# An encoder's self-attention output projection: seven block products with left sums summed in memory, in place of a plain product

## The chip, the cores and the metric

The kernel runs on one core of one Trainium2 chip. The metric is the device time of one execution in microseconds (us): the median of three runs before the change is 2370.38 us (2369.58 to 2371.14). One execution was also profiled; it took 2370.06 us, of which 2368.3 us are the span that the profile shows, so 1.8 us lie around it.

Five engines work side by side, each with its own instruction queue that runs in order: PE (TensorE, matrix products, with its weight loads shown as PEld), DVE (VectorE), ACT (ScalarE), POOL (GpSimd) and SP (SyncE, which here only issues transfers). Sixteen DMA engines move the data of the transfers.

## The reference, cut to what matters

A two-layer encoder over 1024 tokens of 1024 channels, all in float32. Layer 0 mixes tokens by self-attention, layer 1 by a pooling mixer; each layer then attends to 256 memory tokens and runs a gated feed-forward part.

```python
def axial_gqa_attention(h, w_qkv, q_gain, k_gain, w_o):
    qkv = h @ w_qkv                      # 16 query heads of 64, 4 key/value heads
    ...
    o = softmax(q k^T) v                 # for each head, 1024 x 64
    return o @ w_o                       # (1024 x 1024) @ (1024 x 1024)

def memory_cross_attention(h, mem_n, w_q, w_kv, w_o):
    q, kv = h @ w_q, mem_n @ w_kv        # mem_n: 256 x 1024, w_kv: 1024 x 2048
    ...

x = x + axial_gqa_attention(rmsnorm(x, g), ...)
x = x + memory_cross_attention(rmsnorm(x, g), ...)
x = x + conv_gated_ffn(rmsnorm(x, g), ...)
```

## The kernel before

**Arithmetic.** A float32 operand is kept as a high part (fp32r, cut by an ACT copy, helper `high`, L620) and a low part (the rest, a DVE subtraction, helper `low`, L623). A product of two such operands takes three matrix instructions (helper `mm3`, L696 to L698: high by high, high by low, low by high). Split operands live in 20 slots `R` of 128 x 2048 numbers, each of two halves. Float32 data on its way is held in a few scratch tiles `scr` of 128 x 1024.

**Stages.** First w_qkv is applied (to 155 us of the span), then attention runs (155 to 428 us), then attention's output projection (`attention_out`, L1944), then layer 0's cross-attention with its query projection, its keys and values, scores and output; then the feed-forward part and layer 1.

**Attention** runs over 16 groups of one half of the tokens (512) and one pair of heads (128 channels): GROUPS goes through the 8 pairs of the first half of the tokens, then through those of the second. Per group PE forms scores (`pT`, L1260), their peaks (`pS`, L742), and the weighted values (`pO`, L1302); ACT takes exponentials (L1267); DVE finds peaks (L748) and adds pairs of exponential tiles (L1313); POOL adds those on (L1318). One group later, `plan_sum` finishes a group: PE sums the exponentials over partitions (L1343), ACT copies the result (L1347), three small transfers and a DVE reciprocal of 8 x 128 (L1356) turn it into a factor, POOL multiplies (L1370), ACT cuts the high parts and POOL subtracts the low parts (L1378). The transposed results of all groups stay in eight `R` slots.

**The output projection** forms 16 products, one for each tile of 128 tokens and each half of the 1024 output columns: 8 steps over the contraction times 3 instructions, 24 instructions of 512 columns each. Each product has a PSUM bank of its own (`pB`); a DVE add (L1990) puts it onto the residual tile `X`, SP saves that to memory, and when both halves of a tile of tokens are there, ACT squares it, POOL takes the root (L669, L671), DVE scales it (L333) and PE transposes it (L339) for the query projection. The left half of the weight is fetched and split during the last but one group of attention, the right half at the start of this stage.

**Seven products.** Other large products of this kernel already use Winograd's form of Strassen's scheme (class `Seven`, table PRODUCTS): left and right are cut into 2 x 2 blocks, seven block products replace eight, and sums of blocks (S1 to S4 on the left, T1 to T4 on the right) are formed beforehand. The banks x, y and z of the table take several products each, one after another; the result is read from the bank between them. `weight_sums` forms the four sums of a weight's blocks on DVE and stores them to memory, `weight_blocks` fetches and splits blocks and sums. Both serve w_o of the cross-attention and the feed-forward's down-projection.

**Order.** `Plan` holds operations with the tiles that they read, write and take. For PE the order is the one in which they are added (lists such as ATT, QKV and OUT); for the other engines it comes out of a planner with costs per kind (KINDS) and due times. `order` rows below show what results.

**The memory's keys and values** of the cross-attention are formed in 8 column blocks of 256: 4 for keys, 4 for values, two products of 24 instructions of 256 columns each (`plan_part`, L1569).

## Time and profile before

| | |
|---|---|
| median of three runs | 2370.38 us |
| the profiled execution | 2370.06 us |
| its span | 2368.3 us |
| DVE busy in the span | 1943.0 us |
| ACT busy in the span | 1235.1 us |
| POOL busy in the span | 407.3 us |
| HBM read, written | 252.17 MB, 95.22 MB |

A row of a timeline gives start, duration, engine, line, operation, output and inputs, and how often, and in brackets the idle time before it and what ended that. A row of the table by windows gives the stretch, its length, then for each engine busy time and instructions, the clock granted to PE as a share of full speed, the share of time that the DMA engines were busy, and GB/s. A row of a group gives busy time, mean duration in ns, idle time before it and what ended it.

### The profile page before, as it was taken

The numbers are of one execution on the slowest core, as the hardware profiler recorded it, in microseconds if no ns is written. First come the engines' busy times: TensorE is split into PE (matmuls) and PEld (weight loads), VectorE is DVE, ScalarE is ACT, GpSimd is POOL, SyncE is SP. The second block draws the span as 40 slices with busy tenths as digits, with TensorE's granted clock in tenths as the row PEclk, the third lists the DMA queues.
The fourth block names the chain that finished last, engine by engine and source line by source line (L and its number), as shares of the span: only waits on it lengthen the run. The fifth ranks groups of instructions, "written<-read, shape, count | busy, mean of one in ns | idle before, by whom it ended". The sixth has DMA issues, their size and how long they took to land.

```text
span 2368.3 us, 33050 instructions
## 1 busy us (share of the span) xinstructions
PE 2352.9 (99%) x11759; PEld 1881.2 (79%) x11759; DVE 1943.0 (82%) x2798; ACT 1235.1 (52%) x2083; POOL 407.3 (17%) x387
## 2 busy tenths in 40 slices
PE   9999999999999999999999999999999999999998
PEld 8764544788988888888888889898888888888887
DVE  6679999578878998888888768978899888888875
ACT  6555556255565654555464427556575544544542
POOL 5677777210110000000000013011000000000001
PEclk9999999999999999999999999999999999999999
DMA  7000002736946243334488643696624333447863
GB/s 259 1 1 15 20 15 55 244 130 214 328 157 214 78 124 89 111 101 118 131 282 286 209 156 132 212 316 214 206 78 123 89 115 104 114 129 236 286 191 103
DMA packets 340721, 354.43 MB, mean 150 GB/s; under 512 B 34532, under 2 KB 259148, under 8 KB 340556
## 3 DMA queue, kind: packets, MB, share of 16 engines
q1 hardware_dynamic: 340412, 352.31, 46.0%
q8 instruction: 93, 1.52, 0.3%
q14 instruction: 72, 0.59, 0.1%
q10 hardware_dynamic: 144, 0.00, 0.0%
HBM read 252.17 MB, written 95.22 MB: 147 GB/s over the span
## 4 chain that ended last, share of the span: by engine, by line
PE 92%; DVE 4%; DMA 1%; ACT 1%; issue 1%; POOL 0%; SPq 0%; POOLq 0%; DVEq 0%; ACTq 0%
PE pB L696 23%; PE pB L698 23%; PE pB L697 23%; PE pO L1302 4%; PE pT L1260 4%; PE pA L696 3%; PE pA L698 3%; PE pA L697 3%; DVE R L623 2%; PE pS L742 2%; ACT R L620 1%; PE pS L1343 1%; PE pB L339 0%; DMA scr<-Gs 0%; PE pA L2489 0%
## 5 line engine op out<-in xcount | busy, mean ns | idle before, releaser
L697 PE MATMUL pB<-R,R 128*128 128x512 f32 (+1 forms) x2656 | 1000.2, 377 | 0.3 <-DVE R L623 0.2
L696 PE MATMUL pB<-R,R 128*128 128x512 f32 (+1 forms) x2594 | 981.3, 378 | 3.6 <-DVE X L2179 1.3
L698 PE MATMUL pB<-R,R 128*128 128x512 f32 (+1 forms) x2594 | 975.7, 376 | 0.6 <-DVE R L623 0.6
L697 PEld LDWEIGHTS pB<-R,R 128*128 128x128 f32 x2656 | 500.2, 188 | 92.1 <-DVE R L623 2.6
L696 PEld LDWEIGHTS pB<-R,R 128*128 128x128 f32 x2594 | 488.6, 188 | 96.6 <-ACT R L620 4.6
L698 PEld LDWEIGHTS pB<-R,R 128*128 128x128 f32 x2594 | 488.3, 188 | 90.1 <-DVE R L623 1.4
L620 ACT ACTIVATE R<-scr 128x512 fp32r<-128x512 f32 (+3 forms) x438 | 299.1, 716 | 261.3 <-DMA scr<-Gs 63.1
L623 DVE TENSOR_TENSOR R<-scr,R 128x512 fp32r<-128x512 f32 (+3 forms) x402 | 320.5, 826 | 34.1 <-ACT R L620 33.4
L669 POOL TENSOR_SCALAR ms<-ss 128x1 f32<-128x1 f32 x52 | 19.7, 379 | 1645.8 <-ACT R L2471 630.0
L623 DVE TENSOR_TENSOR R<-X,R 128x512 fp32r<-128x512 f32 (+1 forms) x299 | 192.0, 658 | 47.2 <-ACT R L620 46.8
L620 ACT ACTIVATE R<-X 128x512 fp32r<-128x512 f32 (+1 forms) x295 | 177.4, 613 | 95.9 <-PE pB L697 42.3
L407 ACT COPY scr<-pB 128x512 f32<-128x512 f32 x156 | 91.5, 586 | 200.0 <-PE pB L698 199.1
L748 DVE TENSOR_REDUCE nm<-pS 128x1 f32<-128x512 f32 x232 | 148.4, 683 | 20.0 <-PE pS L742 18.1
L1267 ACT ACTIVATE X<-pT 128x1024 f32<-128x1024 f32 x128 | 125.0, 1023 | 72.8 <-PE pT L1260 70.2
L696 PE MATMUL pA<-R,R 128*128 128x512 f32 (+1 forms) x452 | 162.5, 359 | 0.0
L697 PE MATMUL pA<-R,R 128*128 128x512 f32 (+1 forms) x446 | 160.1, 359 | 0.0
L698 PE MATMUL pA<-R,R 128*128 128x512 f32 (+1 forms) x444 | 159.2, 359 | 0.0
L409 DVE TENSOR_TENSOR scr<-pB,scr 128x512 f32<-128x512 f32 x156 | 106.8, 685 | 24.4 <-PE pB L698 24.3
L1302 PE MATMUL pO<-X,XV 128*64 128x512 f32 x512 | 124.1, 605 | 0.0
L2179 DVE TENSOR_TENSOR X<-pB,X 128x512 f32<-128x512 f32 (+1 forms) x110 | 75.1, 684 | 54.9 <-PE pB L698 54.7
L1260 PE MATMUL pT<-R,R 64*128 64x512 f32 x768 | 103.2, 393 | 0.4 <-DVE R L623 0.4
L620 ACT ACTIVATE R<-pB 128x256 fp32r<-128x256 f32 (+1 forms) x144 | 66.4, 492 | 68.2 <-PE pB L698 32.4
(255 smaller groups left out, 2961.2 us busy)
## 6 DMA issues: line engine op xcount, KB each, us to landing
Gs<-X SPq DMA_DIRECT2D x105, 256.0 KB
X<-in_ffn_w_up SPq DMA_DIRECT2D x51, 512.0 KB
scr<-in_ffn_w_down SPq DMA_DIRECT2D x43, 512.0 KB
scr<-Gs SPq DMA_DIRECT2D x35, 512.0 KB
scr<-in_xattn_w_kv SPq DMA_DIRECT2D x32, 512.0 KB
XV<-in_ffn_w_up SPq DMA_DIRECT2D x31, 512.0 KB
scr<-Gs SPq DMA_DIRECT2D x40, 384.0 KB
scr<-in_xattn_w_o SPq DMA_DIRECT2D x24, 512.0 KB
```

The lines of the kernel that those rows point to most:

```text
L407: self.nc.scalar.copy(out, p)
L409: self.nc.vector.tensor_tensor(out=out, in0=p, in1=out, op=OP.add)
L620: self.nc.scalar.activation(hi, src, AF.Copy)
L623: self.nc.vector.tensor_tensor(out=lo, in0=src, in1=hi.bitcast(F32), op=OP.subtract)
L696: mm(out, ah, bh, start=start, stop=False)
L697: mm(out, ah, bl, start=False, stop=False)
L698: mm(out, al, bh, start=False, stop=stop)
L748: nc.vector.tensor_reduce(NM[G][:, 2 * n + x.start:2 * n + x.stop], S, axis=AX.X, op=OP.max, negate=True)
L1260: nc.tensor.matmul(T[G, kt % 2][:, x * 512:(x + 1) * 512], left, right, start=first and (i, j) == (0, 0), stop=shifted or (not first and i ...
L1267: nc.scalar.activation(E[G, kt], T[G, kt % 2], AF.Exp)
L1302: nc.tensor.matmul(O[G][x * HD:(x + 1) * HD], V32[kt // 4][:, kt % 4, m // 4 * 2 + x], E[G, kt][:, x * 512:(x + 1) * 512], start=kt == 0, ...
L2179: nc.vector.tensor_tensor(out=x, in0=banks[k][:, c], in1=x, op=OP.add)
```

## The change

It does five things.

1. **Projection by seven products.** Left is the attention result, cut by halves of the tokens and by even and odd pairs of heads (four pairs each); right is w_o, cut by the same rows and by halves of the columns. For each of four token tiles there are seven products of 4 steps times 3 instructions: 28 products of 12 instructions in place of 16 of 24. Each product is followed by its own DVE add (28 in place of 16).
2. **Left sums in memory.** A new tensor `Sd` in memory holds S3, S4, S1 and S2. Each group, once scaled, is copied with its sign turned (a new ACT instruction, L1389), and then leaves for those sums in which it stands (LEAVES): the first contribution as a plain store from SP, the others as transfers issued from POOL that add to what is in memory. A transfer to a place waits until the one before it to that place has landed. In the projection the sums are fetched and split (8 loads of 512 KB). Blocks A11, A12 and A22 are still split on chip as before, in one piece of 512 columns; A21 is not.
3. **Weight sums.** w_o is fetched, and its sums are formed (16 DVE subtractions) and stored during the w_qkv stage. In the projection the blocks and sums are fetched in four lots.
4. **Order.** GROUPS moves pair 7 of the first half to the very end. The last two groups take their reciprocal on DVE over 128 x 512 at once, without the transfers (`whole`). ATT is new. Query transposes of layer 0 move partly to QUERY, and five of them use one wide bank.
5. **Values of the memory** are formed in 2 column blocks of 512 in place of 4 of 256, in both layers (48 instructions of 512 columns a block in place of 48 of 256); MEMORY writes out their order.

```diff
+SUMS_AT = (1, 3, 5, 7)
+LEAVES = {(0, 0): ((0, 2, 0, 0), (3, 4, 1, 0)), (0, 1): ((1, 2, 0, 1),), (1, 0): ((2, 3, 0, 0), (0, 2, 1, 1), (3, 4, 0, 1)),
+          (1, 1): ((2, 4, 0, 1), (1, 2, 1, 1))}
-GROUPS = [(half, m) for half in range(2) for m in range(NH // 2)]
+GROUPS = [(half, m) for half in range(2) for m in range(NH // 2 - (not half))] + [(0, NH // 2 - 1)]
...
-QUERY = [(2, 0), 5, (1, 0), (2, 1), None], [3, (2, 0), 5, (1, 0), (2, 1), None]
+QUERY = [1, (2, 0), (1, 0), 3, 5, (2, 1), None, (1, 1)], [3, (2, 0), 5, (1, 0), (2, 1), None, (1, 1)]
+ATT = [("X", 1), ("X", 3), ("W", 1), ("S", "S2", 0), ("S", "S2", 1), ("O", 1, 0), ("O", 1, 2), ("O", 1, 1),
+       ("O", 2, 2), ("O", 1, 3), ("O", 2, 0), ("O", 2, 1), ("X", 5), ("W", 2), ("S", "S3", 0), ("O", 2, 3),
+       ("S", "S3", 1), ("X", 7), ("O", 6, 0), ("O", 6, 2), ("O", 6, 3), ("O", 6, 1), ("O", 7, 0), ("O", 7, 2),
+       ("O", 7, 1), ("O", 7, 3), ("W", 3), ("S", "S1", 0), ("S", "S1", 1), ("O", 4, 0), ("O", 4, 2), ("S", "S4", 0),
+       ("S", "S4", 1), ("O", 5, 0), ("Z",), ("O", 3, 0), ("O", 5, 2), ("T", 4), ("E",), ("O", 3, 2), ("T", 0),
+       ("O", 4, 1), ("O", 4, 3), ("O", 5, 1), ("Z",), ("T", 2), ("O", 3, 1), ("Z",), ("T", 6), ("O", 5, 3),
+       ("O", 3, 3), ("Z",)]
...
+                def whole():
+                    nc.vector.reciprocal(ON[G][:, 512:], T.pop(b))
+                def turned():
+                    nc.scalar.activation(ON[G][:, 512:], ON[G][:, :512], AF.Copy, scale=-1.0)
+                def leave(a, b, minus, more):
+                    src, n = ON[G][:, 512 * minus:512 * minus + 512], b - a
+                    out = self.SD[a:b, m // 2].rearrange("n p c -> p n c")
+                    src = src[:, None, :].to_broadcast([P, n, 512])
+                    if more:
+                        nc.gpsimd.dma_start(out=out, in_=src, accum_op=OP.add)
+                    else:
+                        nc.sync.dma_start(out=out, in_=src)
...
+            plan.add("product", 12, emit, ls + ws, [b], [("A" if bank == "x" else "B", b)] if fresh else (), ls + ws + ([] if fresh else [b]))
+            plan.add("add", 512, add, [b, *x], x, uses=[b], late=2.5)
...
-                p = sm[b] = self.psB()[:, :256]
+                p = sm[b] = self.psB()[:, :width]
```

**POOL at the end of attention.** L1318 (now L1331) adds exponential tiles, L1370 (now L1386) scales a group, L1378 (now L1396) forms low parts, L1405 issues an adding transfer. The rows begin with the last adds of the last group but one; behind them a group is finished, and then the next. Before:

```order
L1318 TENSOR_TENSOR scr<-scr 128x1024 x2
L1318 TENSOR_TENSOR scr<-scr,X_1657 128x1024
L1318 TENSOR_TENSOR scr<-scr,X_1658 128x1024
L1370 TENSOR_TENSOR scr<-scr 128x512
L1378 TENSOR_TENSOR R_85<-scr,R_84 128x256
L1378 TENSOR_TENSOR R_71<-scr,R_86 128x256
L1370 TENSOR_TENSOR scr<-scr 128x512
L1378 TENSOR_TENSOR R_85<-scr,R_84 128x256
L1378 TENSOR_TENSOR R_71<-scr,R_86 128x256
```

and now:

```order
L1331 TENSOR_TENSOR scr<-scr 128x1024 x2
L1331 TENSOR_TENSOR scr<-scr,X_1720 128x1024
L1331 TENSOR_TENSOR scr<-scr,X_1721 128x1024
L1386 TENSOR_TENSOR scr<-scr 128x512
L1405 DMA Sd<-scr 128x512
L1405 DMA Sd<-scr 128x2x512
L1386 TENSOR_TENSOR scr<-scr 128x512
L1405 DMA Sd<-scr 128x2x512
L1405 DMA Sd<-scr 128x512
L1396 TENSOR_TENSOR R_74<-scr,R_74 128x512
L1386 TENSOR_TENSOR scr<-scr 128x512
L1405 DMA Sd<-scr 128x512
```

The two low parts of 256 columns became one of 512, or none in the first group finished here, and two transfers stand ahead of it; the last two rows begin the last group of all, with one transfer.

**DVE at the end of attention and the start of the projection.** L1313 (now L1326) and L1318 (now L1331) add exponential tiles, L1356 is the small reciprocal, L1990 (now L2020) is the projection's add. Before:

```order
L1318 TENSOR_TENSOR scr<-scr 128x1024
L1313 TENSOR_TENSOR scr<-X_1657,X_1658 128x1024
L1318 TENSOR_TENSOR scr<-scr,X_1653 128x1024
L1356 RECIPROCAL rs<-rs 8x128 x2
L1990 TENSOR_TENSOR X_1656<-pB,X_1656 128x512
```

and now:

```order
L1331 TENSOR_TENSOR scr<-scr 128x1024
L1326 TENSOR_TENSOR scr<-X_1720,X_1721 128x1024
L1331 TENSOR_TENSOR scr<-scr,X_1716 128x1024
L1383 RECIPROCAL scr<-pS 128x512 x2
L2020 TENSOR_TENSOR X_1719<-pB,X_1719 128x512
```

Two reciprocals of 512 columns, back to back, stand where the two small ones stood.

**DVE in the second half of the projection.** L379 and L1897 are block sums of w_q and of the cross-attention's w_o, L633 forms low parts, L343 scales a finished token tile. The rows begin with the add of product 5 for the first token tile. Now:

```order
L2020 TENSOR_TENSOR X_1720<-pB,X_1720 128x512
L379 TENSOR_TENSOR scr<-scr 128x512 x2
L633 TENSOR_TENSOR R_82<-scr,R_82 128x512
L633 TENSOR_TENSOR R_85<-scr,R_85 128x512
L633 TENSOR_TENSOR R_73<-scr,R_73 128x512
L2020 TENSOR_TENSOR X_1719<-pB,X_1719 128x512
L379 TENSOR_TENSOR scr<-scr 128x512
L343 SCALAR_TENSOR_TENSOR X_1720<-X_1720,rs,scr 128x1024
L2020 TENSOR_TENSOR X_1721<-pB,X_1721 128x512
L633 TENSOR_TENSOR R_73<-scr,R_73 128x512
L633 TENSOR_TENSOR R_70<-scr,R_70 128x512
L343 SCALAR_TENSOR_TENSOR X_1719<-X_1719,rs,scr 128x1024
```

Before, in the middle of the projection (L1880 is now L1897, L333 is now L343):

```order
L1990 TENSOR_TENSOR X_1654<-pB,X_1654 128x512
L1880 TENSOR_TENSOR scr<-scr 128x512 x4
L623 TENSOR_TENSOR R_69<-pB,R_68 128x4x128
L623 TENSOR_TENSOR R_80<-pB,R_77 128x4x128
L333 SCALAR_TENSOR_TENSOR X_1654<-X_1654,rs,scr 128x1024
L1990 TENSOR_TENSOR X_1657<-pB,X_1657 128x512
```

An add used to come once in 24 matrix instructions; it now comes once in 12, with the rows between it and the next little fewer.

More of the change, by code (lines that the diff above doesn't have):

```diff
@@ new lines, in plan_sum @@
+                if G < last - 1:
+                    plan.add("copy", 512, copy, [b, ("on", G)], [own], uses=[b, *used])
+                    plan.add("load", 0.2, spread, [own], [("rs", G)], uses=used)
+                    plan.add("recip", 128, inverse, [("rs", G)], [("rs", G)])
+                    plan.add("load", 0.2, park, [("rs", G)], [("inv", G)])
+                    plan.add("load", 0.5, back, [("inv", G)], [own], uses=used)
+                else:
+                    plan.add("recip", 512, whole, [b, ("on", G)], [own], uses=[b, *used], late=6.0)
@@ new lines, in plan_sum @@
+                plan.add("pool", 512, scale, [own, ("on", G)], [("on", G)], uses=used)
+                plan.add("copy", 512, turned, [("on", G)], [own], uses=used, late=12.0)
+                for a, b, minus, more in LEAVES[half, m % 2]:
+                    plan.add("sum" if more else "load", (b - a) / 4, partial(leave, a, b, minus, more), [own if minus else ("on", G)],
+                             [("SD", x, m // 2) for x in range(a, b)], uses=used, late=14.0)
+                if (half, m % 2) != (1, 0):
+                    k = ("OT", 8 * half + m)
+                    plan.add("copy", 512, partial(part, 0), [("on", G)], [k], [("half", k)], used, late=14.0)
+                    plan.add("pool", 512, partial(part, 1), [("on", G), k], [k], uses=[*used, k], late=15.0)
+                    plan.kept.add(k)
@@ L1950, in attention_out @@
         plan.known.update(self.known)
[L1952 to L1967 removed]
+        of = lambda left, q: (left == "A22") * 8 + 2 * q + (left != "A11")
@@ new lines, in plan_sums, with fetch, high, low @@
+        def plan_sums(name, g):
+            raw, ks, x = ("aoraw", name, g), [("as", name, g, j) for j in range(2)], NAMES.index(name)
+            def fetch():
+                L[raw] = self.scr()
+                nc.sync.dma_start(out=L[raw].rearrange("p (q c) -> p q c", q=2), in_=self.SD[x, 2 * g:2 * g + 2].rearrange("q p c -> p q c"))
+            def high():
+                L[name, g] = R.get_pair()
+                self.high(R.hv(L[name, g][0]), L[raw])
+            def low():
+                self.low(*(R.hv(h) for h in L[name, g]), L.pop(raw))
+            plan.add("load", 1, fetch, [("SD", x, q) for q in (2 * g, 2 * g + 1)], [raw], [("scr", raw)])
+            plan.add("copy", 1024, high, [raw], ks, [("half", k) for k in ks], [raw])
+            plan.add("add", 1024, low, [raw, *ks], ks, uses=[raw, *ks])
+            plan.ended[ks[0]] = lambda: R.put_half(*L.pop((name, g)))
```

199 lines of the change are left out of this document (87 added, 112 removed).

## The prediction

> **What bounds the kernel now.** I read the page's busy times first, then the windows of the stages that the change touches, then timelines inside them.
>
> ```profile
> PE 2352.9 (99%) x11759; PEld 1881.2 (79%) x11759; DVE 1943.0 (82%) x2798; ACT 1235.1 (52%) x2083; POOL 407.3 (17%) x387
> PE 92%; DVE 4%; DMA 1%; ACT 1%; issue 1%; POOL 0%; SPq 0%; POOLq 0%; DVEq 0%; ACTq 0%
> 155.00:428.00 273.00, 271.42 (x1642) 133.20 (x1642) 247.84 (x319) 155.79 (x193) 210.74 (x108) 1.00 0.12 26
> 428.00:552.00 124.00, 123.09 (x574) 101.62 (x571) 82.64 (x120) 49.48 (x88) 14.94 (x22) 1.00 0.57 193
> 475.00:523.00 48.00, 48.00 (x233) 40.13 (x233) 35.59 (x52) 22.79 (x44) 5.81 (x11) 1.00 0.40 135
> 523.00:552.00 29.00, 28.09 (x131) 22.84 (x130) 26.68 (x44) 17.30 (x31) 2.29 (x2) 1.00 0.40 120
> ```
>
> PE is busy 99% of the span and holds 92% of the chain of work that ended last, at the full granted clock (1.00). So a PE instruction less is time won, unless something else becomes late. The third row is attention: DVE is at 247.8 of 273 us and POOL at 210.7, both near full. The fourth runs from the projection's first product to the first finished query block: PE is full, DVE is at 82.6 of 124 us; but in its last 29 us DVE is at 92%, and there alone PE loses 0.9 us. DVE is the engine to watch.
>
> **What goes from PE.** Each product of the projection is followed by a DVE add, whose starts give PE's pace:
>
> ```profile
> 434.23 0.69 DVE L1990 TENSOR_TENSOR X<-pB,X 128x512 f32<-128x512 f32 x1 [0.56 <-PE pB L698]
> 439.67 0.69 DVE L1990 TENSOR_TENSOR X<-pB,X 128x512 f32<-128x512 f32 x1 [4.75 <-PE pB L698]
> 445.11 0.69 DVE L1990 TENSOR_TENSOR X<-pB,X 128x512 f32<-128x512 f32 x1 [4.75 <-PE pB L698]
> 599.58 0.28 PE L696 MATMUL pB<-R,R 128*128 128x256 f32 x1
> ...
> 600.65 0.28 PE L696 MATMUL pB<-R,R 128*128 128x256 f32 x1
> ```
>
> 24 instructions take 5.44 us, 0.2267 us each. 16 x 24 = 384 of them become 28 x 12 = 336: 48 x 0.2267 = **10.9 us less**. The memory's values: nine steps of 256 columns take 1.07 us, 0.119 us each. In two layers 384 x 0.119 = 45.7 us become 192 x 0.2267 = 43.5 us: **2.2 us less**. Together 13.1 us; no other PE instruction is added or lost.
>
> **What is put on DVE in the same place.** Between the projection's first add and the first query block come 12 more adds, 20 low parts of 512 columns for blocks and sums of w_o and 8 of 1024 columns for the left sums, less 4 of 1024 columns that split the right half of w_o before.
>
> ```profile
> 497.39 3.09 DVE L623 TENSOR_TENSOR R<-scr,R 128x512 fp32r<-128x512 f32 x5
> 445.89 1.23 DVE L623 TENSOR_TENSOR R<-scr,R 128x1024 fp32r<-128x1024 f32 x1
> 433.80 0.39 PE L698 MATMUL pB<-R,R 128*128 128x512 f32 x1
> ```
>
> At 0.62 us (3.09 / 5) and 1.23 us that is 32 x 0.62 + 4 x 1.23 = 24.8 us more. The stretch from 434.2 to 552 us had some 82 us of DVE work in 118 us; it would have 107 us in 107. So part of it must be put off (16 weight subtractions are not urgent), and PE will wait for some of the rest. I walk the new order of DVE. Up to 44 us into the projection, adds at 2.72 us intervals leave room for three low parts each, and DVE keeps up. From product 5 on it doesn't, in three ways:
> - Products 5 and 3 of a token tile use one bank, and product 3 may not start before the add of product 5 has read it. Twice they stand back to back on PE. The add starts 0.43 us after the start of a product's last instruction (434.23 - 433.80) and takes 0.69 us; PE would have gone on after 0.23 us. So 0.43 + 0.69 - 0.23 = 0.9 us, twice: **1.8 us**.
> - From the add of product 5 (tile 4) on, 8 DVE instructions (that add among them), 5.3 us, and the scaling, 1.3 us, stand ahead of the scaled tile that PE transposes, and the add waits for PE; PE reaches the transpose 5.4 us after product 5. With the 0.9 us above PE waits about 0.4 us; the second back-to-back pair finds DVE some 0.7 us late, the last transposes 0.4 us.
> - Then comes the stretch in which DVE was at 92%. I take 1.0 us more than before.
> The last two together **2.5 us**; bounds are 0 (the 0.9 us that PE lost at 92% stays all there is) and 8 us (no subtraction is put off, and DVE works at its 92%: 107 / 0.92 - 107 = 9.3 us, less the 1.8 us already taken, rounded up).
>
> **The end of attention.** In the last two groups the reciprocal is taken over 512 columns.
>
> ```profile
> L1356 DVE RECIPROCAL rs<-rs 8x128 f32<-8x128 f32 x16 | 14.9, 932 | 5.3 <-DMA rs<-scr 5.3
> L1626 DVE RECIPROCAL inv<-sum 128x4 f32<-128x4 f32 x16 | 2.8, 175 | 13.3 <-ACT X L1621 8.9 <-ACT XV L1621 3.6 <-POOL X L1630 0.8
> 425.29 1.23 DVE L1318 TENSOR_TENSOR scr<-scr,X 128x1024 f32<-128x1024 f32 x1
> 428.56 0.59 ACT L1347 COPY scr<-pS 128x512 f32<-128x512 f32 x1 [2.01 <-PE pS L1343]
> 436.03 1.29 POOL L1370 TENSOR_TENSOR scr<-scr 128x512 f32<-128x512 f32 x1 [11.93 <-DMA inv<-rs]
> 440.76 1.49 SPq L1958 DMA_DIRECT2D scr<-in_attn_w_o  x3
> ```
>
> From 4 to 128 columns it grows by 757 ns, 6.1 ns a column, so 512 take 0.175 + 508 x 0.0061 = 3.3 us. Both follow the last exponential add, which ends at 426.5 us: 429.8 and 433.1 us. POOL then scales the first group (1.3 us), issues two transfers, forms its low part (1.3 us, as L1370) and scales the second group. If a transfer holds POOL for d = 1 us, that ends at 435.8 us; ACT's copies of 0.59 us (sign, then high part) end at 437.1 us, and after one more transfer and 1.3 us the low part is there at 438.4 us. Before, 22 us of other products hid this; now product 2 needs them after three products and nine steps, at 428.4 + 45 x 0.2267 = 438.6 us, and the low part at 439.1 us. So it costs nothing up to d of about 1.2 us, and 3 us per us above. The trace has no transfer issued by POOL: SP holds its queue 0.5 us for one (1.49 / 3), a POOL pass over 128 x 512 takes 1.3 us, and one over 1024 columns 2.4 us (below). I take it near the POOL pass, 1.3 to 1.4 us: **0.5 us**, bounds 0 and 3 x (2.4 - 1.2) = 3.6 us.
>
> [...]
>
> **POOL inside attention** must take up the other transfers.
>
> ```profile
> 278.16 1.30 POOL L1370 TENSOR_TENSOR scr<-scr 128x512 f32<-128x512 f32 x1 [1.02 <-DMA scr<-inv]
> 280.75 2.52 POOL L1378 TENSOR_TENSOR R<-scr,R 128x256 fp32r<-128x256 f32 x2 [1.29 <-ACT R L620]
> 283.23 2.37 POOL L1318 TENSOR_TENSOR scr<-scr 128x1024 f32<-128x1024 f32 x1
> 286.82 2.39 POOL L1318 TENSOR_TENSOR scr<-scr 128x1024 f32<-128x1024 f32 x1 [1.23 <-DVE scr L1313]
> 289.29 4.84 POOL L1318 TENSOR_TENSOR scr<-scr,X 128x1024 f32<-128x1024 f32 x2
> 295.14 1.29 POOL L1370 TENSOR_TENSOR scr<-scr 128x512 f32<-128x512 f32 x1 [1.02 <-DMA scr<-inv]
> ```
>
> A group takes 17.0 us (295.14 - 278.16). Adds take 9.6 us, scaling 1.3; the low parts shrink from 2.5 us to 1.3 in one group of two and to none in the other: 11.6 us of work on average. That leaves 5.4 us for two transfers, d up to 2.7 us if no wait remains. Cost nothing; beyond that, see the rivals. ACT's sixteen sign copies, 0.6 us each, go beside PE, since ACT is at 156 of 273 us.
>
> **Transfers, and the w_qkv stage.** The left sums' last contributions leave at about 433 us. A load on the chain shows how long one may take at worst:
>
> ```profile
> 675.16 3.96 DMA X<-Xq
> 1207.70 6.07 DMA scr<-Gs
> 450.00:460.00 10.00, 10.00 (x46) 8.29 (x45) 6.87 (x9) 1.06 (x1) 0.00 (x0) 1.00 0.96 358
> ```
>
> With 4 to 6 us to land, 4 us to fetch and 2.3 us to split, S2 is there at 443 to 446 us; product 6 needs it at 428.4 + 8 x 2.72 = 450.2 us. SP's queue waits meanwhile, and the weight blocks behind it: 7.1 MB for products 6 and 7 then move at the 358 GB/s shown in 20 us, to 457 to 459 us; product 7 needs its last block, split, at about 463 us. Cost nothing; at the stage's mean of 193 GB/s they would take 37 us, to 474 to 476 us, and cost some 12, the far bound. The 16 DVE subtractions during w_qkv (11 us in 95 with DVE at 65 to 70%) may each be in PE's way briefly: **0.3 us**, bounds 0 and 1.
>
> **The sum**, against the profiled execution's 2370.06 us: -13.1 + 1.8 + 2.5 + 0.5 + 0.3 = -8.0, so **2362.0 us**. The median of runs is 2370.38 us, 0.3 us above, and my chances are against it; 0.2% of it (4.7 us), about what a measurement here can tell from no change, puts "faster" below 2365.6 us.
>
> **Rivals.**
> - *All of it arrives.* The waits of DVE are taken up by instructions put off: for it, the 16 subtractions (11 us) can slip by 20 us and more; against it, the back-to-back products. 2370.1 - 13.1 + 0 to 3 = 2357 to 2359.5 us. Chance 0.22.
> - *My forecast*, 2359.5 to 2365 us: 0.45.
> - *The gain is nearly given back.* DVE becomes the bound from product 5 to the query blocks (8 us in place of 2.5), or the blocks land late (3 to 5 us at a rate between the two rows): 2365 to 2371 us, about 2367.5. For it, 107 us of DVE work in 107. Chance 0.24, a quarter of it still "faster".
> - *Slower: the adding transfers hold POOL.* Beyond d = 2.7 us POOL falls behind by 2 x (d - 2.7) in each of eight groups of the second half; the sums that PE waits for and scratch tiles come late, and the chain at the end adds 3 x (d - 1.2). It ends over 0.2% slower from 16 x (d - 2.7) + 3 x (d - 1.2) = 13 us, d = 3.1 us; at d = 4 us the loss is 29 us, 2391 us. Against it, no POOL row takes that long but the 2.4 us passes. Chance 0.09.
> - That the change doesn't do what it says I leave out: the new order has 240 PE instructions less, as counted above.
>
> [...] What DVE runs in attention:
>
> ```profile
> L748 DVE TENSOR_REDUCE nm<-pS 128x1 f32<-128x512 f32 x232 | 148.4, 683 | 20.0 <-PE pS L742 18.1
> L1313 DVE TENSOR_TENSOR scr<-X,X 128x1024 f32<-128x1024 f32 x46 | 77.6, 1687 | 1.5 <-ACT X L1267 0.8 <-POOL R L1378 0.6
> 400.54 1.21 DVE L1313 TENSOR_TENSOR scr<-X,X 128x1024 f32<-128x1024 f32 x1
> ```
>
> [...]
>
> **How the numbers follow.** The likeliest case gives 2362.0 us. The range takes in the first three cases to where the DVE bound of 8 us and late blocks meet: 2356.5 to 2369 us; outside are the slower case and the far ends. Faster 0.22 + 0.45 + 0.06 = 0.73, same 0.18, slower 0.09.
>
> **What would show it.** PE instructions 48 x 512 fewer in the projection, 192 fewer over the two layers' values; the projection's products 2.72 us apart up to product 4, then gaps of 0.9 us ahead of product 3, put down to DVE L2020; DVE over 90% busy for the 90 us from product 5 on; POOL's idle time in attention shrunk, its groups still 17.0 us. It is wrong if PE waits at product 2 for the last group (d over 2 us), at products 6 or 7 for transfers, or if groups of the second half grow longer.

## The result, and the profile after

The changed kernel takes 2384.51 us (median of 6 runs, 2383.41 to 2386.97) against 2369.98 us for the kernel before (6 runs, 2369.01 to 2371.14): 1.0063 times as long, 95% interval 1.0050 to 1.0076. It is slower by 14.5 us; the forecast was 8 us less. Two executions among all those told of below, of 2683.68 and 3924.25 us at a granted clock of 0.88 and 0.556, are counted in no median here. The profiled execution of the changed kernel took 2383.8 us with a span of 2382.0 us, 13.7 us more than before. Two lines of the page of the changed kernel, the busy time of each engine (with share of the span, and instructions) and the shares of the chain of work that ended last:

```profile
PE 2348.0 (99%) x11519; PEld 1862.8 (78%) x11519; DVE 1988.6 (83%) x2838; ACT 1254.2 (53%) x2089; POOL 422.7 (18%) x387
PE 88%; DVE 5%; DMA 3%; ACT 1%; issue 1%; POOL 1%; SPq 0%; DVEq 0%; POOLq 0%; ACTq 0%
```

The 240 PE instructions are gone, as counted. But PE's busy time fell by 4.9 us in place of 13.1, and 4% of the chain went from PE to transfers, DVE and POOL. Where this came about is read from three starts on PE: the first score product, the first product of the projection, the first product of the cross-attention's keys. Timeline of before, PE:

```profile
153.55 0.86 PE L1260 MATMUL pT<-R,R 64*128 64x512 f32 x6
428.44 0.50 PE L696 MATMUL pB<-R,R 128*128 128x512 f32 x1
```

(the keys' row, at 599.58 us, stands in the prediction), and of the changed kernel:

```profile
157.89 0.86 PE L1273 MATMUL pT<-R,R 64*128 64x512 f32 x6
436.45 0.50 PE L706 MATMUL pB<-R,R 128*128 128x512 f32 x1
615.44 0.28 PE L706 MATMUL pB<-R,R 128*128 128x256 f32 x1
```

| stage, us | before | changed | difference | forecast |
|---|---|---|---|---|
| to the first score product | 153.6 | 157.9 | +4.3 | +0.3 |
| attention, to the projection's first product | 274.9 | 278.6 | +3.7 | 0 |
| projection and query projection, to the keys | 171.1 | 179.0 | +7.9 | -6.1 |
| the rest | 1768.7 | 1766.6 | -2.1 | -2.2 |

Only the last row came as forecast. The table of what PE waited for in the third stage (engine, tile, line, and what it waited for: us in total, times, longest):

```profile
PE pA L708 <- POOL R L1396: 8.1, 1, 8.1
PE pB L706 <- DVE XV L361: 2.1, 1, 2.1
PE pB L706 <- DVE R L633: 1.5, 1, 1.5
PE pB L707 <- DVE R L633: 1.5, 1, 1.5
PE pB L706 <- DVE X L2020: 0.9, 1, 0.9
PE pB L706 <- DVE XV L2020: 0.8, 1, 0.8
```

and the windows of attention, and of the projection and query projection up to the first query block:

```profile
158.00:436.00 278.00, 274.45 (x1652) 133.59 (x1648) 249.43 (x327) 160.54 (x195) 209.29 (x109) 1.00 0.31 62
436.00:563.00 127.00, 112.07 (x506) 90.30 (x503) 102.55 (x144) 62.75 (x107) 20.83 (x23) 0.96 0.68 233
```

POOL's busy time in attention is what it was, and DVE is busy for 102.6 of 127 us behind it. One of PE's waits is longer than the others of the table together, and it is for a low part that POOL forms. The timeline of PE and of POOL around it:

```profile
447.02 0.39 PE L707 MATMUL pA<-R,R 128*128 128x512 f32 x1
455.55 0.80 PE L708 MATMUL pA<-R,R 128*128 128x512 f32 x1 [8.14 <-POOL R L1396]
456.14 0.63 PE L706 MATMUL pB<-R,R 128*128 128x512 f32 x1
456.57 0.63 PE L707 MATMUL pB<-R,R 128*128 128x512 f32 x1
...
440.32 2.17 POOL L1405 DMA_DIRECT2D Sd<-scr  x2 [1.89 <-DMA Sd<-scr]
441.67 2.13 POOL L1396 TENSOR_TENSOR R<-scr,R 128x512 fp32r<-128x512 f32 x1
442.93 2.12 POOL L1386 TENSOR_TENSOR scr<-scr 128x512 f32<-128x512 f32 x1
453.32 0.88 POOL L1405 DMA_DIRECT2D Sd<-scr  x1 [8.26 <-DMA Sd<-scr]
453.94 1.55 POOL L1396 TENSOR_TENSOR R<-scr,R 128x512 fp32r<-128x512 f32 x1
```

The last group is scaled by 445 us. Its adding transfer then waits 8.26 us, until the transfer of the group before to the same place has landed, and the low part that PE needs stands behind it in POOL's queue. PE stands still for 8.1 us. Behind that it starts 12 instructions 0.43 us apart in place of 0.227 (456.57 - 456.14): 2.4 us more, and 0.4 us at the restart. The granted clock of the stage is 0.96; from 455.5 to 461 us, the stretch of these 12 instructions, it is 0.50, and 0.427 us is a little under twice 0.227 us.

### The profile page after: what moved, and what is told of

It is laid out like the page before. It is cut to its first block, busy times and chain, and to the rows that moved or that the text cites. A ratio compares the mean times of both kernels' runs of the same rounds, so it can differ in the third digit from the quotient of the medians.

```text
span 2382.0 us, 32810 instructions
## 1 busy us (share of the span) xinstructions
PE 2348.0 (99%) x11519; PEld 1862.8 (78%) x11519; DVE 1988.6 (83%) x2838; ACT 1254.2 (53%) x2089; POOL 422.7 (18%) x387
## 3 DMA queue, kind: packets, MB, share of 16 engines
q0 software_dynamic: 3904, 7.34, 2.1%
## 4 chain that ended last, share of the span: by engine, by line
PE 88%; DVE 5%; DMA 3%; ACT 1%; issue 1%; POOL 1%; SPq 0%; DVEq 0%; POOLq 0%; ACTq 0%
PE pB L706 22%; PE pB L708 22%; PE pB L707 22%; PE pO L1315 4%; PE pA L708 4%; PE pA L706 4%; PE pA L707 4%; PE pT L1273 4%; PE pS L752 2%; DVE R L633 1%; DMA scr<-in_attn_w_qkv 1%; ACT R L630 1%; DMA Sd<-scr 0%; DMA scr<-in_xt 0%; PE pS L1356 0%
## 5 line engine op out<-in xcount | busy, mean ns | idle before, releaser
L707 PE MATMUL pB<-R,R 128*128 128x512 f32 (+1 forms) x2553 | 974.3, 382 | 1.9 <-DVE R L633 1.8
L706 PE MATMUL pB<-R,R 128*128 128x512 f32 (+1 forms) x2507 | 961.8, 384 | 7.3 <-DVE XV L361 2.9
L708 PE MATMUL pB<-R,R 128*128 128x512 f32 (+1 forms) x2495 | 951.8, 381 | 0.4 <-DVE R L633 0.4
L707 PEld LDWEIGHTS pB<-R,R 128*128 128x128 f32 x2553 | 480.9, 188 | 93.9 <-DVE R L633 4.1
L706 PEld LDWEIGHTS pB<-R,R 128*128 128x128 f32 x2507 | 472.1, 188 | 103.4 <-issue 7.0
L708 PEld LDWEIGHTS pB<-R,R 128*128 128x128 f32 x2495 | 469.7, 188 | 92.0 <-DVE R L633 1.8
L630 ACT ACTIVATE R<-scr 128x512 fp32r<-128x512 f32 (+3 forms) x446 | 311.8, 729 | 274.6 <-DMA scr<-Gs 66.6
L633 DVE TENSOR_TENSOR R<-scr,R 128x512 fp32r<-128x512 f32 (+3 forms) x430 | 341.4, 823 | 42.6 <-ACT R L630 41.7
L633 DVE TENSOR_TENSOR R<-X,R 128x512 fp32r<-128x512 f32 (+1 forms) x299 | 191.9, 657 | 46.1 <-ACT R L630 45.8
L708 PE MATMUL pA<-R,R 128*128 128x512 f32 (+1 forms) x458 | 165.1, 360 | 8.1 <-POOL R L1396 8.1
L706 PE MATMUL pA<-R,R 128*128 128x512 f32 (+1 forms) x468 | 169.1, 361 | 0.4 <-ACT XV L1638 0.4
L707 PE MATMUL pA<-R,R 128*128 128x512 f32 (+1 forms) x468 | 168.8, 361 | 0.0
L708 PEld LDWEIGHTS pA<-R,R 128*128 128x128 f32 x458 | 86.6, 189 | 21.3 <-POOL R L1396 8.6
```

What stands on the lines that cost most here:

```text
L630: self.nc.scalar.activation(hi, src, AF.Copy)
L633: self.nc.vector.tensor_tensor(out=lo, in0=src, in1=hi.bitcast(F32), op=OP.subtract)
L706: mm(out, ah, bh, start=start, stop=False)
L707: mm(out, ah, bl, start=False, stop=False)
L708: mm(out, al, bh, start=False, stop=stop)
```

## The experiments

Sixteen kernels; times are medians beside runs of the kernel before on the same chip (2369.2 to 2369.7 us). A stage's length is that of one execution; attention took 279.7 and 282.3 us in two of the kernels below that are written alike up to its end, so a difference of 1 us in it says nothing.

**The order on POOL.** In the last two groups the low part goes ahead of the transfers:

```diff
+low = [("OT", 8 * half + m)] if G >= last - 1 else []
+if low:
+    plan.add("copy", 512, partial(part, 0), [("on", G)], low, ...)
+    plan.add("pool", 512, partial(part, 1), [("on", G), *low], low, ...)
 for a, b, minus, more in LEAVES[half, m % 2]:
-    plan.add("sum" if more else "load", ..., [own if minus else ("on", G)],
+    plan.add("sum" if more else "load", ..., [own if minus else ("on", G), *low],
```

> In the last two groups of attention the high and low parts are formed ahead of the adding transfers, on POOL and on ACT; nothing else changes. Theory A: the 8.1 us that PE waits in the fourth product of the projection come from one adding transfer of the last group, which stands on POOL ahead of the low part that PE needs and waits 8.3 us until the previous transfer to the same place has landed; the fall of the clock behind it (12 instructions at 0.43 us in place of 0.23) costs 2.4 us more, and 0.4 us go at the restart. Then PE's wait there is under 1 us, the granted clock stays at 1.00, and the time falls by 10 to 11 us, to 2373 to 2375 us. Rival: the transfers hold POOL and the DMA engines so long that the low part comes late in any order (the loads of the token tiles share the engines): PE still waits 4 us or more, the time falls by 5 us at most.

2385.07 us (ratio 1.0067, 1.0054 to 1.0080): nothing was gained, and both theories as written fell (the rival's numbers came, no gain and a wait of over 4 us, but not its late low part). The wait for POOL is gone, but another of the same size took its place. PE's waits in that stage, in this kernel (its L2025 is L2020 of the changed one, its L1990 L1985, its L1946 L1941):

```profile
PE pA L706 <- DVE X L2025: 8.7, 2, 7.3
```

and the timelines of SP, DVE and PE:

```profile
439.62 0.46 SPq L1946 DMA_DIRECT2D scr<-Wa  x1
450.00 0.36 SPq L1990 DMA_DIRECT2D scr<-Sd  x1
452.10 6.64 SPq L1946 DMA_DIRECT2D scr<-Wa  x2
...
452.37 1.23 DVE L633 TENSOR_TENSOR R<-scr,R 128x1024 fp32r<-128x1024 f32 x1 [6.42 <-ACT R L630]
463.18 0.69 DVE L633 TENSOR_TENSOR R<-scr,R 128x512 fp32r<-128x512 f32 x1 [4.85 <-ACT R L630]
463.79 0.68 DVE L2025 TENSOR_TENSOR X<-pA,X 128x512 f32<-128x512 f32 x1
...
464.53 0.79 PE L706 MATMUL pA<-R,R 128*128 128x512 f32 x1 [7.26 <-DVE X L2025]
```

SP stands from 440 to 450 us at the fetch of S2, whose last contribution has not landed. The weight blocks behind it come late, so do their low parts on DVE, and behind one of those stands the add that frees the bank PE needs. The same landing now holds up SP, DVE and PE in place of POOL and PE.

**Without the adding transfers:** `for a, b, minus, more in [z for z in LEAVES[half, m % 2] if not z[3]]:`

> All 20 adding transfers are left out, so that the left sums in memory hold their first contribution only; sign copies, plain stores, loads and products stay. Theory A gives the same 10 to 11 us as in the run with the low parts first. Attention, from its first score product to the projection's first product, took 278.1 us in place of 274.5: if the transfers cause these 3.6 us (they take POOL 2.2 us in a row in some groups, so that its adds fall together with DVE's and both are slower), attention comes back to about 275 us and the time is about 2371 us. Rival: sign copies on ACT, the two large reciprocals and the new order cause them; then attention still takes 277 to 278 us, and the time is about 2374 us.

2369.02 us (0.9998, 0.9989 to 1.0007), 15.5 us less than the changed kernel and 2 us below what was written: the adding transfers cost more than the whole loss. The three starts on PE in this kernel:

```profile
158.40 0.86 PE L1273 MATMUL pT<-R,R 64*128 64x512 f32 x6
432.66 0.50 PE L706 MATMUL pB<-R,R 128*128 128x512 f32 x1
600.49 0.28 PE L706 MATMUL pB<-R,R 128*128 128x256 f32 x1
```

Attention takes 274.3 us, so its 3.7 us are theirs too, and the third stage 167.8 us in place of 179.0. In the fourteen versions here that have adding transfers, the changed kernel among them, attention takes 277.7 to 282.3 us.

**The same transfers, not adding:** `nc.gpsimd.dma_start(out=out, in_=src)` in place of the same with `accum_op=OP.add`.

> The changed kernel with the same 20 transfers from POOL, to the same places in the same order and with the same waits, but overwriting in place of adding, so that each left sum holds its last contribution only. Theory F: the adding makes the landings long (a read and a write for each piece): landings of 3 to 5 us inside attention, 5 to 8 us at its end, PE's wait for the low part 2 to 5 us in place of 8.1, and the time 2376 to 2381 us; attention still takes about 278 us, since POOL issues as many transfers. Rival: any transfer from POOL lands so late beside the loads (371 GB/s): the landings stay at 10 to 11.6 us, the wait at 7 us or more, the time within 2 us of 2384.5.

2375.55 us (1.0026, 1.0017 to 1.0035), 9 us less. The view of line L1405 (instruction duration in ns, least, median, most; then the time to landing) in the changed kernel:

```profile
L1405 POOL DMA_DIRECT2D Sd<-scr x20: 867/1220/1432, 215.9 to 453.3; - x20
DMA to landing us min/median/max: 4.0/6.0/11.6
```

and with plain transfers:

```profile
L1405 POOL DMA_DIRECT2D Sd<-scr x20: 569/588/792, 215.5 to 443.3; - x20
DMA to landing us min/median/max: 2.3/3.3/7.2
```

POOL's queue on the page (packets, MB, time of its packets as a share of the engines'), changed kernel:

```profile
q0 software_dynamic: 3904, 7.34, 2.1%
```

and with plain transfers:

```profile
q0 software_dynamic: 2112, 7.34, 0.8%
```

Here adding doubled POOL's time for a transfer (1220 ns against 588), nearly doubled packets (3904 against 2112) and time to landing (6.0 us against 3.3), and took 2.6 times as much of the DMA engines (2.1% against 0.8%). PE's wait for the low part falls to 2.0 us. Theory F holds but in one point (the time lies a little under what was written); that the adding reads and writes each piece, which it names as the cause, is not shown. Attention, from 157.42 us to

```profile
432.31 0.50 PE L706 MATMUL pB<-R,R 128*128 128x512 f32 x1
```

takes 274.9 us, as before the change, not 278: those 3.7 us are a loss of the adding, not of twenty transfers as such.

**Without the token tiles' loads** at the end of attention (`self.load_x(t)` left out for tiles 0 to 4 and 6):

> The changed kernel without the six loads of token tiles 0 to 4 and 6... of the residual that are asked for at the end of attention and at the start of the projection (3 MB; the residual of tiles 0, 1, 2, 3, 4 and 6 is then whatever stands in the tile). Theory A, on why landings take 10 to 11.6 us there when they take 4 to 8 us inside attention: the transfers share the DMA engines with these loads (371 GB/s, share 1.02). Then the landings at 428 to 453 us of the span fall to 4 to 8 us, PE's wait of 8.1 us for the low part to 2 to 5 us, and the time to 2376 to 2381 us. Rival: the landing time belongs to the transfers themselves (the longest are those of two places, issued back to back): landings stay at 10 us, the wait at 7 us or more, the time within 2 us of 2384.5.

2381.13 us (1.0048, 1.0034 to 1.0062), 3.4 us less. The time to landing of line L1405's transfers between 424 and 460 us, in this kernel:

```profile
DMA to landing us min/median/max: 5.6/8.4/9.4
```

and PE's wait:

```profile
PE pA L708 <- POOL R L1396: 4.0, 1, 4.0
```

In the changed kernel the same stretch has 4.4, 10.2 and 11.6 us. So the loads lengthened the landings by 2 us (medians, 10.2 against 8.4 us), and PE's wait halves, from 8.1 to 4.0 us; without the adding the landings are 5.8 us there, 4.4 us less.

**The planner told of the landing** (low parts first, and `"sum": ("POOL", 1.0, 0.0, 12.0)` in place of 4.0):

> As the run with the low parts first, and the planner is told that an adding transfer lands 12 us after it was issued, not 4: the second half of S2 is now fetched and split later, behind weight blocks on SP and behind adds on DVE. Theory A, mended: the wait for a landing (10 to 11.6 us at the end of attention, 4 to 8 us before) holds up whatever stands behind it in an in-order queue: POOL's low part in the changed kernel, and with the low parts first SP's weight blocks (SP waits 10 us for the landing) and with them DVE's low parts and adds, for whose banks PE waits 8.7 us. Then the longer of the two waits (7.3 us) and the slow clock behind it go; the first half of S2, whose load takes 12 us to land, still stands ahead of an add: 1 to 3 us of waiting stay. 2375 to 2378 us. Rival: the DMA engines are full there (371 GB/s), and the transfers come late in any order: PE waits as long for weight blocks or sums, 2383 to 2386 us.

2381.42 us (1.0045, 1.0032 to 1.0057). The third stage falls to 172.3 us, and the wait for that add to 1.2 us, as forecast. But attention grew to 282.2 us, since its order came out otherwise too (PE waits 3.3 us there for a sum of exponentials). The time is above the 2375 to 2378 us written down.

**Two late groups** (low parts first as well):

```diff
-GROUPS = [(half, m) for half in range(2) for m in range(NH // 2 - (not half))] + [(0, NH // 2 - 1)]
+GROUPS = [(half, m) for half in range(2) for m in range(NH // 2) if half or m not in (5, 7)] + [(0, 5), (0, 7)]
```

> As the run with the low parts first, and the last two groups of attention are pairs 5 and 7 of the first half of the tokens, which stand in one left sum only (S4, needed last), so that the transfers into S2 leave a group earlier, 17 us. Theory A, mended: no landing is then waited for ahead of work that PE needs; PE's waits in the first half of the projection fall from 8.7 us to under 2 us, the clock stays, and the time is 2373 to 2376 us. Rival (full DMA engines: the six token tiles, S2 and the weight blocks are asked for within 20 us): waits of 5 us or more stay, 2380 us or more.

2376.50 us (1.0029, 1.0018 to 1.0041), 8 us less, 0.5 us above what was written for theory A. PE's waits in the first half of the projection are one of 1.5 us (L2025 is L2020 of the changed kernel):

```profile
PE pA L706 <- DVE X L2025: 1.5, 1, 1.5
```

The DMA engines are as busy all the same (1.03 of their time between 446 and 456 us, 333 GB/s). What cost 8 to 11 us was the place of the landing in the order; the load of the engines alone did not.

**The w_qkv stage.** Subtractions left out (`if name != "Wa":` ahead of the add):

> The 16 subtractions that form the sums of w_o during the w_qkv stage are left out; its loads and its stores stay, so the stored blocks are the plain ones. Theory C: DVE, busy 95 to 100% between 55 and 75 us of the span, makes PE late there by 3.6 us (transposes of the key differences, peaks, query products); without the subtractions the first score product comes 3 to 4 us earlier, at about 154.5 us in place of 158.3, and the time is about 2381 us. Rival: the loads and stores do it (they hold scratch tiles and stand in SP's queue ahead of the pieces of w_qkv): the first score product stays after 157 us, the time within 1 us of 2384.5.

2380.22 us (1.0047, 1.0034 to 1.0060), and the first score product at 153.74 us: all but 0.2 of the 4.3 us are DVE's work, as theory C has it. The windows from 55 to 75 us, before:

```profile
55.00:65.00 10.00, 10.00 (x53) 8.38 (x52) 6.40 (x16) 3.57 (x8) 9.66 (x13) 1.00 0.00 1
65.00:75.00 10.00, 10.00 (x48) 8.18 (x47) 4.50 (x12) 7.72 (x25) 6.84 (x4) 1.00 0.00 0
```

and changed:

```profile
55.00:65.00 10.00, 8.92 (x45) 7.17 (x43) 9.96 (x18) 3.21 (x7) 8.78 (x11) 1.00 0.53 197
65.00:75.00 10.00, 9.89 (x48) 8.05 (x49) 9.05 (x17) 5.13 (x16) 6.98 (x7) 1.00 0.94 330
```

DVE (third pair) goes from 6.4 and 4.5 us of ten to 10.0 and 9.1, and PE (first pair) loses 1.2 us in these two windows alone.

**Other places for them.** `SUMS_AT = (7, 9, 11, 13)`, in attention `late=22.0` for the transfers, no sign copy where nothing reads it; on top of two late groups:

> As the run with two late groups, and three changes more, each read in its own stage: the sums of w_o are formed behind query products 7, 9, 11 and 13 in place of 1, 3, 5 and 7; inside attention the transfers may be issued 8 us later, which puts most of them behind the first of POOL's additions of the group; the sign copy that nothing reads is left out. Theory C (amount of DVE work at 55 to 87 us): the first score product comes at 154 to 155.5 us in place of 158. Theory B (two transfers in a row put POOL's addition into DVE's): attention takes 275 to 276.5 us in place of 277.8. Together 2370 to 2374 us in place of 2376.5. Rivals: the subtractions cost the same wherever they stand in that stage (first score product at 157 us or later); the transfers cost by their sum and not by their place (attention 277.5 us or more); with both 2376 us.

2374.51 us (1.0024, 1.0015 to 1.0034). First score product at 155.14 us, but attention takes 279.7 us; together the projection begins at 434.81 us in place of 435.10. Theory C holds, theory B doesn't; why attention grew is not shown.

The same with `SUMS_AT = (1, 5, 9, 13)` and `late=18.0`:

> As the mended run, with the sums of w_o behind query products 1, 5, 9 and 13, and the transfers of attention allowed 4 us later in place of 8, which keeps them in front of POOL's additions. Theory C: spread out they cost DVE's room nowhere: first score product at 154 to 156 us. Theory B: with the transfers in front of the additions again, attention takes 277 to 278 us. Rival for C: a set at 55 us already costs 1.5 us or more (156 us or later); rival for B: 276 us or less here too, so that what helped was the sign copies left out.

2377.45 us (1.0030, 1.0017 to 1.0042); first score product at 156.59 us, attention 281.0 us. Spread out they cost more, and this attention was no shorter; both theories on place fell.

On POOL, behind query products 5, 7, 9 and 11 (`(nc.gpsimd if name == "Wa" else nc.vector).tensor_tensor(...)`), with two late groups and one set of other sums moved (below):

> As that run, with the 16 subtractions that form the sums of w_o put on POOL, behind query products 5, 7, 9 and 11, where POOL is busy 50 to 60% of the time. Theory C (it is DVE's time that PE waits for in that stage): the first score product comes 2 to 4 us earlier, at 154 to 156 us, and the time is 2368 to 2371 us. Rival: POOL takes 1.3 us for each and stands in the same chains (roots and rotated queries), so PE waits for POOL in place of DVE: first score product at 158 us or later, no gain or a loss.

2371.34 us (1.0006, 0.9997 to 1.0015), 3.1 us less than the kernel with the sums on DVE behind products 1, 3, 5 and 7 (2374.48 us, below); first score product at 155.46 us, 1.9 us earlier. POOL takes the sums without a wait of PE that the trace shows, but the edit moved them as well, and on DVE behind 7, 9, 11 and 13 the start was 155.14 us. So it does not tell place from engine; that the loss of the stage is DVE's time rests on the run without the subtractions.

**The query stretch.** All of `("Z",)` moved from ATT to MEMORY:

> The changed kernel with the 16 subtractions for the cross-attention's w_o moved out of the projection and the query stretch into the stage of the memory's keys and values. Theory D: PE's three waits at the end of the query transposes (2.1, 1.5 and 1.5 us, for DVE's differences and low parts) are a matter of how much DVE has to do: it is 93% busy there, and six of the subtractions (3.6 us) stand in that stretch. Then those waits fall to 2 us or less in all, and the time by 3 to 4 us, to 2380 to 2382 us. Rival: they are the length of the chain behind the last transposes (copy, difference, high part, low part), whatever else DVE does: the waits stay at 4 us or more and the time within 1 us of 2384.5. The two waits of 0.9 us ahead of product 3 stay in both.

2390.74 us (1.0086, 1.0073 to 1.0100). In the stretch theory D nearly holds: the waits of 2.1, 1.5 and 1.5 us became 1.3, 0.4 and 0.3, with a new one of 0.6. But the time rose by 6 us in place of falling by 3 to 4: everything behind the keys' first product takes 1775.6 us in place of 1766.6: PE waits there 4.7 us for a weight's high part and 1.5 us for an add. The work was moved to a worse place.

Only the last of the four sets moved, to behind the scores of tile 1, on top of the run with `SUMS_AT = (7, 9, 11, 13)`:

> As the mended run, and the last four of the subtractions for the cross-attention's w_o moved from the end of the query stretch to the end of the stage of the memory's values. Theory D: PE's waits at the last query transposes (2.3 and 1.7 us, 1.6 us of slow clock) fall by 2 to 3 us, nothing comes back later as it did when all sixteen were moved, and the time is 2 to 3 us under that of the mended run. Rival: the last four lie behind the waits already, or the moved ones delay weights or banks in the scores' stage: no gain, or a loss there of the same size.

2371.52 us (1.0009, 1.0000 to 1.0018), 3.0 us less than without that edit, and the waits at the last transposes are 1.1, 0.9 and 0.4 us: theory D.

The same without putting off transfers and with `SUMS_AT = (1, 3, 5, 7)`:

> The run with two late groups, the sign copy that nothing reads left out, and the last four subtractions for the cross-attention's w_o moved to the end of the values' stage; the w_o sums stand where the change put them (query products 1, 3, 5 and 7), and the transfers of attention are not put off. Theory B mended (the transfers cost attention by their sum, not by their place): from the start to the projection's first product as with two late groups, 435 to 436.5 us, and the time 2370 to 2373 us, as with the transfers put off. Rival: putting them off and moving the sums did help by 1 to 2 us, hidden by scatter: 2373 to 2375 us here.

2374.48 us (1.0023, 1.0013 to 1.0032): the rival's time. Yet the projection begins at 436.75 us, against 436.73 us in the run before; the 3 us by which that one is faster stand in the third stage (165.5 us against 171.1), not where the edit was, and what makes them is not shown.

**Products 5 and 3 apart:** `("O", 5, 0), ("Z",), ("O", 5, 2), ("O", 3, 0)` and `("O", 5, 3), ("Z",), ("O", 3, 1), ("T", 6), ("O", 3, 3)`.

> The changed kernel with another product between product 5 and product 3 of the first and of the last token tile. Theory E: PE waits there for the add that reads the shared bank, 1.04 and 0.95 us; with another product between, both waits go and the time falls by 1.5 to 2 us, to about 2382.7 us. Rival: DVE is late by then anyway, so that the waits come back a product or two later, or at the transposes: no change beyond 0.5 us.

2389.04 us (1.0080, 1.0067 to 1.0093), 4.5 us more, 2.1 of them in the third stage. The waits ahead of product 3 are gone, and new ones stand at the transposes:

```profile
PE pB L349 <- DVE X L343: 4.1, 1, 4.1
PE pA L349 <- DVE X L343: 2.6, 1, 2.6
```

DVE is late there in any case: the rival had the mechanism right, but it wrote down no change, and the time rose.

**The values alone,** on the kernel before:

> The kernel before with one part of the change alone: the memory's values in two blocks of 512 columns, with the written-out order of that stage. Expected from 192 instructions of 0.2267 us in place of 384 of 0.119 us: 2.2 us less, 2367.8 us. Rival: the wider products need their weights and banks at other times, and PE waits for splits; then the gain is given back and the time is 2369 to 2371 us.

2369.63 us (1.0000, 0.9991 to 1.0009). The stretch behind the keys' first product is shorter by 1.4 us in its profile (1767.3 us), by 2.1 us in the changed kernel's; the time doesn't tell it from no change.

**All mends together** (the run with the sums on POOL, and `late=22.0`):

> All mends together: low parts first, two late groups, the sign copy that nothing reads left out, w_o's sums on POOL, four subtractions moved, and the transfers of attention allowed 8 us later. If putting the transfers off helps by 3 us, as the two runs that differ in it and in the sums' place seemed to say: 2367 to 2369.5 us, no worse than before. If that was scatter: 2370.5 to 2372.5 us, as with the sums on POOL alone.

2372.68 us (1.0011, 1.0002 to 1.0020), 1.3 us more than without `late=22.0`: putting the transfers off gains nothing here. The third stage is down to 167.9 us, against 171.1 before the change, but 7.8 us are lost ahead of it (the projection begins at 436.21 us in place of 428.44). No version beat the kernel before; the one with the sums on POOL comes nearest, at 1.0006.

## Why the prediction was wrong

- **What goes from PE** was right: 240 instructions, and behind the keys -2.1 us for -2.2.
- **The end of attention** is the step that failed: "So it costs nothing up to d of about 1.2 us, and 3 us per us above." It let a transfer cost POOL its issue, d. That was 1.17 us on average, less than the 1.3 to 1.4 us taken, so by this step PE would not have waited at all. But each adding transfer also waits on POOL until the one before it to its place has landed. The description of the change says so, and the sum left it out. The landings waited for took 10 to 11.6 us, and the term was 8.1 us of waiting and 2.8 us of restart and slow clock, 10.9 us in place of 0.5.
- **Transfers:** "With 4 to 6 us to land" nearly held inside attention (median 5.8 us, at most 7.9) and failed at its end (median 10.2 us). With the low part out of the way, the fetch of S2 held up SP and DVE for as long: the second half of the same error.
- **POOL inside attention,** "Cost nothing", was wrong by 3.7 us with d far below 2.7 us. That adding costs it is shown (274.3 us without transfers, 274.9 with plain ones). In the second half of the tokens, where a group has two adding transfers, four groups in a row take 17.1, 17.7, 17.2 and 17.6 us (315.78 to 385.37 us); they take 17.0 us each before the change. The sign named for it, "if groups of the second half grow longer", came, though POOL still stands idle for 15 us in these 69.6 us: its room did not run out. How is only argued. POOL's first addition behind the transfers and DVE's sum beside it come late together in the group of 17.7 us:

```profile
338.65 3.18 POOL L1331 TENSOR_TENSOR scr<-scr 128x1024 f32<-128x1024 f32 x1
340.03 2.90 DVE L1326 TENSOR_TENSOR scr<-X,X 128x1024 f32<-128x1024 f32 x1
```

where they take 2.4 and 2.2 us before the change. The mean over attention says nothing of it: DVE's sum took 1640 ns here, 1507 without transfers and 1580 with plain ones, but 1687 before the change, with an attention of 274.9 us. At the end of attention PE also waits once, for 1.5 us, for ACT's exponentials. They stand behind the new sign copy, which waits for POOL's scaling:

```profile
427.81 0.63 ACT L1389 ACTIVATE scr<-scr 128x512 f32<-128x512 f32 x1 [2.90 <-POOL scr L1386]
428.34 1.92 ACT L1280 ACTIVATE X<-pT 128x1024 f32<-128x1024 f32 x2
...
429.40 0.96 PE L1273 MATMUL pT<-R,R 64*128 64x512 f32 x6 [1.54 <-ACT X L1280]
```

The prediction let the sign copies "go beside PE"; it looked at how busy ACT is, not at what a copy waits for.

- **The w_qkv stage:** 0.3 us, bounds 0 and 1, became 4.3. The mean load of DVE over the stage (65 to 70%) was taken for the load where the work lands.
- **DVE in the projection:** the two waits ahead of product 3 were right in place and size (0.9 and 0.8 us, 1.0 each with the restart). The query stretch was under-sized: 5.1 us of waits against 0.9 us before, where 2.5 us were taken in all; the 4.2 us more lie inside the bounds that were given. That it is DVE's load is shown by the moved sums (with all four sets moved, the waits of 2.1, 1.5 and 1.5 us became 1.3, 0.4 and 0.3, with a new one of 0.6).
- **The rivals.** "Slower: the adding transfers hold POOL" had the culprit and the sign, but asked for d over 3.1 us. Its price went by the time that POOL is busy, where the time until landing counted. The d measured is 1.17 us; the landings waited for took 10 to 11.6 us.

By stages the forecast missed by 4.0 us (w_qkv), 3.7 (attention), 14.0 (projection and query projection) and 0.1, together 21.8. Of the 14.0 us, 10.4 are the end of attention (8.1 + 2.8 - 0.5), 1.7 the query stretch (5.6 us by starts, less 1.4 before, less the 2.5 taken), 0.2 the two waits ahead of product 3; the last 1.7 us are gaps of 0.2 us or less. The loss is shown to be the adding transfers' (15.5 us of time) and, apart from them, that of the subtractions (4.3 us); together they are more than the 14.5 us, since products were saved on PE.

## What to carry to other kernels

Here a wait in an in-order queue was priced by what it waited for, and by what stood behind it (8.26 us on POOL, for a landing, became 8.1 us on PE): for each transfer that waits for another, ask when that one lands at the load of that moment, and whose work queues behind. Moving the wait from one queue to another left its cost the same here (8.1 us on POOL, 8.7 us behind SP); what helped was other work ahead of it, a whole group of attention (1.5 us of waiting were left). Read the load of an engine in the 10 us where new work falls, not over its stage. Part of what the products saved on PE was paid for on DVE, which splits and adds (4.3 us in the w_qkv stage, 4.2 us more of waits in the query stretch); look for the same where that engine is as full as DVE was here (92% busy before the change, in the last 29 us of the stretch to the first query block).

## What the hardware showed that was not expected

A transfer from POOL that adds in memory held POOL 1.22 us (median) against 0.59 us for the same transfer without adding, made 3904 packets in place of 2112 for the same 7.34 MB, and landed in 6.0 us in place of 3.3; beside loads (390 to 420 GB/s from 437 to 443 us) it took up to 11.6 us. After a standstill of 8.1 us PE ran 12 instructions at half its clock (0.427 us apart in place of 0.227, granted clock 0.50); after one of 7.3 us, with the low parts first, 7 (0.43 us apart, from 465.12 us on); after one of 2.1 us in the changed kernel, at 544.28 us, none (0.23 us apart). Yet the expectation of the run with one set of sums moved counts, for the run that it builds on, 1.6 us of slow clock at waits of 2.3 and 1.7 us. No run here shows what decides between the two.
